# Multi-query attention with exponentials on two engines: the first and the last tiles of VectorE are scheduled otherwise

## The chip, the core and the metric

The kernel runs on one core of a Trainium2 chip. The metric is the device time of one execution in microseconds (us), the median of three runs. A core has TensorE (matrix products), ScalarE (here exponentials), VectorE and GpSimd (elementwise work) and SyncE, which here only starts transfers. The profile calls them PE, ACT, DVE, POOL and SP.

## What is computed

Attention with 16 query heads that share one head of keys and values, for 8 batches of 1024 positions and a head size of 64:

```python
q: (8, 1024, 16, 64)   k, v: (8, 1024, 64)      # float32
scores   = q @ k.T / sqrt(64)
weights  = exp(scores - max(scores))
weights  = weights / sum(weights)
attn_out = weights @ v
```

The kernel leaves out the subtraction of the maximum, which cancels in the division. It gets the sum from two extra columns beside the values, so that one matrix product gives both the weighted values and the sum.

## The kernel before

Heads are taken in 64 pairs. A pair has 8 tiles of 128 keys, so there are 64 x 8 = 512 tiles; a tile has two halves of 512 queries, for both heads: 1024 units of 128 x 1024 scores. TensorE computes a unit with two matmuls into one of three score buffers in PSUM:

```python
sc[t, c] = psp.tile([P, 2, QC], FP32, tag=f"sc{s}", ...)       # s is 0, 1 or 2
for h in range(2):
    nc.tensor.matmul(sc[t, c][:, h, :], <keys>, <queries>, start=True, stop=True, ...)
```

A tile then goes to one of two engines. ScalarE takes one instruction per unit:

```python
ins = nc.scalar.activation(out=w, in_=sc.pop((t, c)), func=EXP, scale=ascale).ins
```

VectorE has no exponential. It writes the scaled score as a 16-bit integer `z` (two instructions per tile, one per unit), whose bits, read as a half-precision number, are a rough power of two. Two corrections are made from it in further steps:

```python
z = scale * score + offset                     # exp_dve: L534, 128 x 1024, reads PSUM
...
steps[t] = (
    e  = z & 0xFC00                            # 0: L551
    m  = z & 1023 | 14 << 10                   # 1: L554
    m  = m * m, the first 1216 columns         # 2: L546; the other 832 by GpSimd in two pieces
    m  = z * m                                 # 3: L558
    m  = m * m, whole                          # 4: L546, in place of 2
    e  = e + m                                 # 5: L560, only for the last tiles
)
```

(The listing is shortened: each line stands for one instruction.) The exponential of such a tile is the sum of three terms, each with a factor. The sum isn't formed; TensorE multiplies each term by values that carry its factor and adds all three up in PSUM:

```python
TERMS = (1.0, 1.017578125, 0.66650390625)
w = (wt[t], zs[t].bitcast(FP16), ms[t])[k] if t in zs else wt[t]
for y in range(x, x + STEP):                   # STEP = 2 matmuls of 128 x 65
    nc.tensor.matmul(acc[p, grp][...], w[...], kst[p // HP]["v"][...][:, j, 0 : D + 1], ...)
```

So a tile on ScalarE costs 16 value matmuls, one on VectorE 48. For each batch the values are scaled for the three terms; in batch 0 VectorE does it, later GpSimd. The products of a pair are collected in three groups (blocks 0 to 6, 6 to 10, 10 to 16), each in one of two accumulators, and VectorE ends a group with a reciprocal (`rec`, L601) and a product (`norm`, L610).

The last 29 tiles (`MERGE`) are treated apart in this version: VectorE squares the whole of `m` itself, adds two of the three terms, and TensorE multiplies only two, one of them by a fourth scaled copy of the last batch's values:

```python
def terms(t):
    return len(TERMS) if t in vtiles and t < NT - MERGE else 1 + (t in vtiles)
```

Which tile goes to which engine, and the order of the instructions on each, comes from `plan`. When the program is built, it goes through the work with estimated durations and always takes next what can start next. Excerpts:

```python
pe = act = dve = 0.0                           # when each engine is free, in the plan
...
if (not vunits and nt < NT - LAST and zfree
        and todo < (BACKLOG if rest > END else BACK_END)):
    vtiles.add(nt)                             # the next tile goes to VectorE
...
n = NT if nt >= NT - SPLIT else nt + 1 if nt > 1 else nt + FIRST
units = [(t, c) for c in range(2) for t in range(nt, n)]      # for ScalarE
...
if free and vunits and gap >= 3 and not zs and dve <= T + PE_L + 0.4 and act > T + ACT_P:
    kind = "z"                                 # the next score is VectorE's
...
lag = min(LAG, END_LAG + (LAG - END_LAG) * rest / END, RAMP * nq / (2 * NKT))
```

At the very start, the first keys and queries are turned on TensorE, and VectorE makes the copies for it (L478 to L500, and L486) ahead of its first step of an exponential.

Of the kernel before, what the change touches and what calls it, by code (L numbers as in the profile page):

```python
# [10 lines left out]
FP16 = mybir.dt.float16  # L11
# [5 lines left out]
P = 128  # L17
ONE = 1024.0
C0 = 0.4578223016
TERMS = (1.0, 1.017578125, 0.66650390625)  # L20
C1, TERMS1 = 0.3051040521, (1.0, 1.52734375)

ACT_P, ACT_L = 0.905, 1.19
QK_P, AV_B, AV_1, SWITCH, PE_L = 0.22, 0.0295, 0.02, 0.10, 0.49
MARGIN, WAIT = 0.318, 0.144
END, END_LAG = 6.0, 0.037
VEC = dict(z=1.13, rec=0.11, val=0.34)
NORM = 0.07, 0.067
STEPS = (0.6, 0.6, 0.7, 1.13)
MERGE, ADD = 29, 1.13  # L30
WHOLE, QUEUE = 1.13, 3
PIECE, PIECE_T, PIECE_AGE = 416, 1.2, 11.627
VEC_L = 0.19
VEC_DEP = 0.12
BACKLOG, BACK_END = 8.353, 2.46
LAST, SPLIT, FIRST = 12, 8, 3
RAMP, VALS, COLD, WARM = 0.584, 3.0, 1, 0.0
BUSY = 20, 3, 5, 0
WBUFS = 23
ZBUFS = 6  # L40
LAG = 2.1
# [4 lines left out]
def follows(x, y):  # L46

    if x is None or y is None:
        return False
    if len(x) == 5:  # L50
        return len(y) == 5 and x[1] == "norm" and y[1] == "rec" and x[2:] == y[2:]
    if len(x) != 2 or len(y) != 2:
        return False
    if y[0] == "z":
        return x in ((y[1], 0), (y[1], 1))
    return x[0] == y[0] and (x[1], y[1]) in ((2, 1), (4, 1), (3, 2), (3, 4), (5, 3))

def plan(NP, NKT, HP=8):

    NT = NP * NKT
    size = [BLOCKS[g + 1] - BLOCKS[g] for g in range(3)]

    def terms(t):
        return len(TERMS) if t in vtiles and t < NT - MERGE else 1 + (t in vtiles)

    def term(t, k):  # L70
        return len(TERMS) if k == 1 and t >= NT - MERGE else k

    def vec(k, g):
        return NORM[0] + NORM[1] * size[g] if k == "norm" else VEC[k]
# [16 lines left out]
            squared.append((t + PIECE_T, x[2]))  # L91

    squared: list = []
    pe = act = dve = 0.0
    mode = ""
    slot = [0.0] * 3
    acc = [0.0] * 2
# [18 lines left out]
    while p < NP or groups:  # L116
        assert min(pe, dve) < 2e3
        if pe <= dve:
            T = pe
            rest = (2 * NT - nq) / (2 * NKT)  # L120
            if not units and nt < NT and (
                len(aring) < WBUFS or used[aring[-WBUFS]] > 2.9
            ):
                todo = (
                    sum(STEPS[n] if n < 4 else ADD for _, n in steps)
                    + sum(vec("norm", x[3]) + vec("rec", x[3]) for x in evs)
                    + VEC["z"] * (len(zs) + len(vunits))
                )
                zfree = len(vring) < ZBUFS or used[vring[-ZBUFS]] > 2.9
                if (  # L130
                    not vunits and nt < NT - LAST and zfree
                    and todo < (BACKLOG if rest > END else BACK_END)
                ):
                    vtiles.add(nt)
                    vring.append(nt)
                    vunits = [(nt, 0), (nt, 1)]
                    ring.append(nt)
                    nt += 1
                n = NT if nt >= NT - SPLIT else nt + 1 if nt > 1 else nt + FIRST
                aring += range(nt, n)  # L140
                ring += range(nt, n)
                units = [(t, c) for c in range(2) for t in range(nt, n)]
                nt = n
            if nt // NKT >= HP * nb - 3 and nb * HP < NP:
                pool += [(T, "val", nb, k) for k in range(len(TERMS) + (HP * (nb + 1) == NP))]
                nb += 1
            cold = COLD if T < WARM else 1
            free = [s for s in range(3) if slot[s] <= T + (SWITCH if mode != "qk" else 0)]
# [11 lines left out]
            for grp in groups:  # L160
                gp, gg, left, a, n, known = grp
                for t in ring[NKT * gp + known : NKT * (gp + 1)]:
                    left += [
                        (t - NKT * gp, k, x) for k in range(terms(t))
                        for x in range(BLOCKS[gg], BLOCKS[gg + 1], STEP)
                    ]
                    grp[5] += 1
                for j, k, x in left:
                    t = NKT * gp + j
                    if t in vtiles:  # L170
                        r = ready.get((t, k, "v"), FAR)
                    else:
                        r = max(ready.get((t, c), FAR) for c in ((0,), (0, 1), (1,))[gg])
                    r = max(r, vdone.get((gp // HP, term(t, k)), FAR))
                    if n == 0:
                        r = max(r, acc[a])
                    if r < tav and (tav > T or grp is groups[0]):
                        tav, pick = r, (grp, (j, k, x))
# [39 lines left out]
            elif do == "av":  # L218
                st = max(T + (SWITCH if mode != "av" else 0), tav)
                pe, mode = st + cost + (AV_1 if mode == "qk" else 0), "av"  # L220
                grp, (j, k, x) = pick
                gp, gg, left, a, n, known = grp
                t = NKT * gp + j
                left.remove((j, k, x))
                end = known == NKT and not left
                emit(st, "av", gp, gg, j, k, x, n, end, a)
                grp[4] += 1
                share = STEP / size[gg] / terms(t)
                nv += share
                used[t] += share  # L230
                if end:
                    acc[a] = FAR
                    evs.append((pe + PE_L, "rec", gp, gg, a))
                    groups.remove(grp)
            else:
                nxt = [x for x in slot + acc + [tav] if T < x < FAR] + [dve] * (dve > T)
                pe = max(min(nxt, default=0.0), T + 1e-3)
        else:
            T = dve
            over = nt >= NT - LAST and not vunits and not zs  # L240
            beside(T, 0.0 if over else PIECE_AGE, ("sq", "val"))
            steps += [(x[1], len(STEPS) - 1) for x in squared if x[0] <= T]
            squared = [x for x in squared if x[0] > T]
            z = [x for x in zs if x[0] <= T + 0.25]
            todo = [("ev", x) for x in evs if x[0] <= T]
            todo += [("val", x) for x in vals if x[0] <= T][:1]
            if nt > NT - MERGE:
                steps.sort()
            todo += [("step", x) for x in steps if x == min(y for y in steps if y[0] == x[0])][:2]
            free = [x for x in todo if not follows(x[1], last)]  # L250
            late = VEC_DEP if not free else 0.0
# [30 lines left out]
                last = None  # L282
            elif what == "step":
                steps.remove(x)
                dve = T + late + (STEPS[x[1]] if x[1] < 4 else ADD)
                if x[1] == len(STEPS) - 2:
                    if x[0] >= NT - MERGE or sum(y[1] == "sq" for y in pool) > QUEUE:
                        x, dve = (x[0], len(STEPS)), T + late + WHOLE
                        steps.append((x[0], len(STEPS) - 1))
                    else:  # L290
                        pool += [(dve, "sq", x[0], n) for n in range(2)]
                emit(T + late, "step", *x)
                if x[0] >= NT - MERGE:
                    if x[1] == 3:
                        steps.append((x[0], 5))
                    elif x[1] == 5:
                        ready[x[0], 0, "v"] = dve + VEC_L
                elif x[1] in (0, len(STEPS) - 1):
                    ready[x[0], x[1] and len(TERMS) - 1, "v"] = dve + VEC_L
                last = x  # L300
            else:
                nxt = [x[0] for x in zs + evs + vals + squared if x[0] > T] + [pe + 1e-6] * (pe > T)
                dve = max(min(nxt, default=0.0), T + 1e-3)
                last = None
# [7 lines left out]
def kernel(  # L312
# [31 lines left out]
        [consts.tile([P, NKT, D + 2], FP16, name=f"vals{i}_{n}") for n in range(len(TERMS))]  # L344
        for i in range(2)
    ]
    NV = NP * NKT - MERGE
    assert NV >= NP * NKT - HP * NKT
    vals[(B - 1) % 2].append(consts.tile([P, NKT, D + 2], FP16, name="vals_last"))
    for x in vals:  # L350
        for y, c in zip(x, TERMS + TERMS1[1:]):
            nc.gpsimd.memset(y[:, :, D : D + 2], c)

    wbuf = [consts.tile([P, 2, S], FP16, name=f"w{i}") for i in range(WBUFS)]
# [41 lines left out]
    def scale_v(b, k, engine):  # L396

        kst[b]["v"] = vals[b % 2]
        return engine.tensor_scalar(
            out=vals[b % 2][k][:, :, 0:D], in0=kst[b]["vn"], scalar1=(TERMS + TERMS1[1:])[k], scalar2=None,  # L400
            op0=ALU.mult)

    def trans_k(b):
# [121 lines left out]
    def exp_dve(t, c):  # L525

        name = f"{t}"  # L530
        if c == 0:
            zs[t] = dvp.tile([P, 2, S], U16, tag="z", bufs=ZBUFS, name=f"z{name}")
        z = zs[t]
        yield nc.vector.tensor_scalar(  # L534
            out=z[:, :, c * QC : (c + 1) * QC], in0=sc.pop((t, c)), scalar1=vscale,
            scalar2=(15 + math.log2(C0 if t < NV else C1)) * ONE, op0=ALU.mult, op1=ALU.add,
        )
        if c == 0:
            return
# [5 lines left out]
        def square(engine, a, b):  # L545
# [3 lines left out]
        squares[t] = square  # L549
        steps[t] = (  # L550
            lambda: V.tensor_scalar(  # L551
                out=wt[t].bitcast(U16), in0=z, scalar1=0xFC00, scalar2=0 if t < NV else 512,
                op0=ALU.bitwise_and, op1=ALU.bitwise_or),
            lambda: V.tensor_scalar(  # L554
                out=m.bitcast(U16), in0=z, scalar1=1023, scalar2=14 << 10,
                op0=ALU.bitwise_and, op1=ALU.bitwise_or),
            lambda: square(V, 0, 2 * S - 2 * PIECE),
            lambda: V.tensor_tensor(out=m, in0=z.bitcast(FP16), in1=m, op=ALU.mult),  # L558
            lambda: square(V, 0, 2 * S),
            lambda: V.tensor_tensor(out=wt[t], in0=wt[t], in1=m, op=ALU.add),  # L560
        )

    def beside(op, t, n):
# [14 lines left out]
    def value(p, grp, j, k, x, n, end, s):  # L578
# [6 lines left out]
        for y in range(x, x + STEP):  # L585
# [1 line left out]
            o = (y - BLOCKS[grp]) * (D + 1)  # L587
            nc.tensor.matmul(  # L588
                acc[p, grp][:, o : o + D + 1], w[:, h, i * P : (i + 1) * P],
                kst[p // HP]["v"][len(TERMS) if k == 1 and t >= NV else k][:, j, 0 : D + 1],  # L590
                start=(n == 0 and y == x), stop=end, skip_group_check=True,
            )

# [123 lines left out]
```

The softmax here doesn't subtract the row's maximum and nothing guards it: scores larger than these inputs give would overflow.

## Time and profile before

| | |
|---|---|
| device time, median of 3 (lowest, highest) | 754.85 us (754.26, 755.1) |
| span of the profiled execution | 753.1 us |
| TensorE matmul / weight load busy | 734.1 us / 490.7 us |
| ScalarE busy | 741.2 us |
| VectorE busy | 708.9 us |
| GpSimd busy | 330.0 us |
| granted TensorE clock | 1.000 |

The span runs from the first to the last instruction of one execution. A line of a timeline gives the start and the duration in us, the engine, the line of the kernel, the operation, what it writes and reads, and in brackets the engine's idle time ahead of it with the instruction that ended the wait. Numbers behind names count the program's buffers: `sc_1_214` is the 214th tile made, a score of the second half (`1`). ScalarE's outputs `w_98` to `w_120` are a ring of 23 buffers.

### The profile page before, as it was taken

The numbers are of one execution on the slowest core, as the hardware profiler recorded it, in microseconds if no ns is written. First come the engines' busy times: TensorE is split into PE (matmuls) and PEld (weight loads), VectorE is DVE, ScalarE is ACT, GpSimd is POOL, SyncE is SP. The second block draws the span as 40 slices with busy tenths as digits, with TensorE's granted clock in tenths as the row PEclk, the third lists the DMA queues.
The fourth block names the chain that finished last, engine by engine and source line by source line (L and its number), as shares of the span: only waits on it lengthen the run. The fifth ranks groups of instructions, "written<-read, shape, count | busy, mean of one in ns | idle before, by whom it ended". The sixth has DMA issues, their size and how long they took to land.

```text
span 753.1 us, 30241 instructions
## 1 busy us (share of the span) xinstructions
PE 734.1 (97%) x13724; PEld 490.7 (65%) x13724; DVE 708.9 (94%) x1054; ACT 741.2 (98%) x808; POOL 330.0 (44%) x392
## 2 busy tenths in 40 slices
PE   7899999999999999999999999999999999999997
PEld 4455666666666666666666666666666666666666
DVE  6999999999999999999999999999999999998973
ACT  7999999999999999999999999999999999999996
POOL 2457434473444643446344563345533457233100
PEclk9999999999999999999999999999999999999999
DMA  7564454646656456674546746458653566643223
GB/s 132 97 108 88 87 105 87 108 95 105 114 108 105 98 83 108 119 122 88 93 77 122 134 86 103 69 108 134 114 92 83 85 128 115 86 93 79 63 71 96
DMA packets 179888, 75.08 MB, mean 100 GB/s; under 512 B 78384, under 2 KB 178736, under 8 KB 179760
## 3 DMA queue, kind: packets, MB, share of 16 engines
q1 hardware_dynamic: 140544, 54.01, 32.4%
q0 software_dynamic: 37744, 18.36, 21.2%
q8 instruction: 107, 1.75, 0.9%
q10 hardware_dynamic: 1472, 0.79, 0.4%
q14 instruction: 21, 0.17, 0.1%
HBM read 39.58 MB, written 33.55 MB: 97 GB/s over the span
## 4 chain that ended last, share of the span: by engine, by line
ACT 94%; PE 3%; DVE 2%; issue 0%; POOL 0%; DVEq 0%; POOLq 0%
ACT w_109 L519 4%; ACT w_110 L519 4%; ACT w_105 L519 4%; ACT w_112 L519 4%; ACT w_115 L519 4%; ACT w_104 L519 4%; ACT w_117 L519 4%; ACT w_116 L519 4%; ACT w_114 L519 4%; ACT w_106 L519 4%; ACT w_118 L519 4%; ACT w_111 L519 4%; ACT w_102 L519 4%; ACT w_113 L519 4%; ACT w_103 L519 4%; ACT w_107 L519 4%
## 5 line engine op out<-in xcount | busy, mean ns | idle before, releaser
L507 PEld LDWEIGHTS <-k2t_137 64*128 64x128 f16 x256 | 13.7, 94 | 19.4 <-issue 11.5
L507 PEld LDWEIGHTS <-k2t_14688 64*128 64x128 f16 x256 | 12.7, 93 | 11.0 <-issue 4.1
L507 PEld LDWEIGHTS <-k2t_1160 64*128 64x128 f16 x256 | 12.3, 93 | 10.7 <-issue 4.3
L507 PEld LDWEIGHTS <-k2t_5644 64*128 64x128 f16 x256 | 12.4, 93 | 8.2 <-issue 1.8
L507 PEld LDWEIGHTS <-k2t_10166 64*128 64x128 f16 x256 | 12.4, 93 | 8.2 <-issue 1.8
L507 PEld LDWEIGHTS <-k2t_7905 64*128 64x128 f16 x256 | 12.4, 93 | 8.2 <-issue 1.8
L507 PEld LDWEIGHTS <-k2t_12427 64*128 64x128 f16 x256 | 12.0, 93 | 8.1 <-issue 1.8
L507 PEld LDWEIGHTS <-k2t_3383 64*128 64x128 f16 x256 | 12.0, 93 | 7.8 <-issue 1.7
L588 PEld LDWEIGHTS <-w_102 128*128 128x128 f16 x288 | 12.9, 97 | 5.4 <-issue 5.4
L588 PEld LDWEIGHTS <-w_106 128*128 128x128 f16 x288 | 13.0, 97 | 4.6 <-issue 4.6
L588 PEld LDWEIGHTS <-w_108 128*128 128x128 f16 x288 | 12.9, 97 | 4.3 <-issue 4.3
L588 PEld LDWEIGHTS <-w_100 128*128 128x128 f16 x288 | 13.0, 97 | 3.9 <-issue 3.9
L588 PEld LDWEIGHTS <-w_104 128*128 128x128 f16 x288 | 12.8, 97 | 4.0 <-issue 4.0
L588 PEld LDWEIGHTS <-w_98 128*128 128x128 f16 x288 | 12.7, 97 | 4.0 <-issue 4.0
L588 PEld LDWEIGHTS <-w_105 128*128 128x128 f16 x288 | 12.8, 97 | 3.4 <-issue 3.4
L588 PEld LDWEIGHTS <-w_119 128*128 128x128 f16 x272 | 12.1, 97 | 4.2 <-issue 4.2
L588 PEld LDWEIGHTS <-w_117 128*128 128x128 f16 x272 | 12.1, 97 | 4.2 <-issue 4.2
L588 PEld LDWEIGHTS <-w_101 128*128 128x128 f16 x288 | 12.7, 97 | 3.1 <-issue 3.1
L588 PEld LDWEIGHTS <-w_99 128*128 128x128 f16 x288 | 12.7, 97 | 3.1 <-issue 2.7
L588 PEld LDWEIGHTS <-w_103 128*128 128x128 f16 x288 | 12.7, 97 | 2.9 <-issue 2.9
L588 PEld LDWEIGHTS <-w_107 128*128 128x128 f16 x288 | 12.6, 97 | 2.9 <-issue 2.9
L588 PEld LDWEIGHTS <-w_110 128*128 128x128 f16 x272 | 12.2, 97 | 3.5 <-issue 3.5
(5591 smaller groups left out, 3706.7 us busy)
## 6 DMA issues: line engine op xcount, KB each, us to landing
qf<-in_q_dram ACTq DMA_DIRECT2D x2, 256.0 KB, 3.7
qn_187<-in_q_dram POOLq DMA_DIRECT2D x1, 512.0 KB, 6.1
qn_328<-in_q_dram POOLq DMA_DIRECT2D x4, 128.0 KB, 3.8
qn_513<-in_q_dram POOLq DMA_DIRECT2D x4, 128.0 KB, 3.0
out_dram<-osb_498 SPq DMA_DIRECT2D x1, 512.0 KB, 3.2
out_dram<-osb_837 SPq DMA_DIRECT2D x1, 512.0 KB, 4.7
qn_1011<-in_q_dram POOLq DMA_DIRECT2D x4, 128.0 KB, 3.1
out_dram<-osb_1151 SPq DMA_DIRECT2D x1, 512.0 KB, 3.2
```

Of the source, the lines that this page charges most:

```text
L507: nc.tensor.matmul(sc[t, c][:, h, :], kst[p // HP]["k2t"][64 * h : 64 * h + 64, key(p // HP, j, h), :], qt[p][64 * h : 64 * h + 64, 4 * c ...
L519: ins = nc.scalar.activation(out=w, in_=sc.pop((t, c)), func=EXP, scale=ascale).ins
L588: nc.tensor.matmul(acc[p, grp][:, o : o + D + 1], w[:, h, i * P : (i + 1) * P], kst[p // HP]["v"][len(TERMS) if k == 1 and t >= NV else k] ...
```

## The change

It undoes the special treatment of the last 29 tiles: no tile of VectorE is merged, all have three terms, the fourth copy of the last batch's values goes, and GpSimd again helps with the squares. This saves VectorE work and lets the plan be simpler. And the plan is told that VectorE is busy with copies until 2.0 in its time, so that ScalarE gets the first three scores and VectorE the fourth; the first scaling of values may be planned from 4.3 on, not from 3.0. The constants that steer the end, the start and the share of VectorE are set anew.

```diff
-C1, TERMS1 = 0.3051040521, (1.0, 1.52734375)
-END, END_LAG = 6.0, 0.037
+END, END_LAG = 5.567, -0.028
-MERGE, ADD = 29, 1.13
-BACKLOG, BACK_END = 8.353, 2.46
-LAST, SPLIT, FIRST = 12, 8, 3
-RAMP, VALS, COLD, WARM = 0.584, 3.0, 1, 0.0
-BUSY = 20, 3, 5, 0
+BACKLOG, BACK_END = 8.576, 2.062
+LAST, SPLIT, FIRST = 13, 7, 3
+RAMP, VALS, COLD, WARM = 0.541, 4.3, 1, 0.0
+BUSY, READY = (20, 3, 5, 0), 2.0
 ...
-    def terms(t):
-        return len(TERMS) if t in vtiles and t < NT - MERGE else 1 + (t in vtiles)
-
-    def term(t, k):
-        return len(TERMS) if k == 1 and t >= NT - MERGE else k
 ...
-    pe = act = dve = 0.0
+    pe, act, dve = 0.0, 0.0, READY
 ...
-                pool += [(T, "val", nb, k) for k in range(len(TERMS) + (HP * (nb + 1) == NP))]
+                pool += [(T, "val", nb, k) for k in range(len(TERMS))]
 ...
-                        (t - NKT * gp, k, x) for k in range(terms(t))
+                        (t - NKT * gp, k, x) for k in range(len(TERMS) if t in vtiles else 1)
 ...
-            over = nt >= NT - LAST and not vunits and not zs
-            beside(T, 0.0 if over else PIECE_AGE, ("sq", "val"))
+            beside(T, PIECE_AGE, ("sq", "val"))
 ...
-            if nt > NT - MERGE:
-                steps.sort()
 ...
-                    if x[0] >= NT - MERGE or sum(y[1] == "sq" for y in pool) > QUEUE:
+                    if sum(y[1] == "sq" for y in pool) > QUEUE:
 ...
-                if x[0] >= NT - MERGE:
-                    if x[1] == 3:
-                        steps.append((x[0], 5))
-                    elif x[1] == 5:
-                        ready[x[0], 0, "v"] = dve + VEC_L
-                elif x[1] in (0, len(STEPS) - 1):
+                if x[1] in (0, len(STEPS) - 1):
                     ready[x[0], x[1] and len(TERMS) - 1, "v"] = dve + VEC_L
 ...
-            lambda: V.tensor_tensor(out=wt[t], in0=wt[t], in1=m, op=ALU.add),
 ...
-                kst[p // HP]["v"][len(TERMS) if k == 1 and t >= NV else k][:, j, 0 : D + 1],
+                kst[p // HP]["v"][k][:, j, 0 : D + 1],
```

More of the change, by code (lines that the diff above doesn't have):

```diff
@@ L55, in follows @@
         return x in ((y[1], 0), (y[1], 1))
-    return x[0] == y[0] and (x[1], y[1]) in ((2, 1), (4, 1), (3, 2), (3, 4), (5, 3))
+    return x[0] == y[0] and (x[1], y[1]) in ((2, 1), (4, 1), (3, 2), (3, 4))
 def plan(NP, NKT, HP=8):
@@ L124, in plan @@
                 todo = (
-                    sum(STEPS[n] if n < 4 else ADD for _, n in steps)
+                    sum(STEPS[n] for _, n in steps)
                     + sum(vec("norm", x[3]) + vec("rec", x[3]) for x in evs)
@@ L173, in plan @@
                         r = max(ready.get((t, c), FAR) for c in ((0,), (0, 1), (1,))[gg])
-                    r = max(r, vdone.get((gp // HP, term(t, k)), FAR))
+                    r = max(r, vdone.get((gp // HP, k), FAR))
                     if n == 0:
@@ L227, in plan @@
                 grp[4] += 1
-                share = STEP / size[gg] / terms(t)
+                share = STEP / size[gg] / (len(TERMS) if t in vtiles else 1)
                 nv += share
@@ L284, in plan @@
                 steps.remove(x)
-                dve = T + late + (STEPS[x[1]] if x[1] < 4 else ADD)
+                dve = T + late + STEPS[x[1]]
                 if x[1] == len(STEPS) - 2:
-                    if x[0] >= NT - MERGE or sum(y[1] == "sq" for y in pool) > QUEUE:
+                    if sum(y[1] == "sq" for y in pool) > QUEUE:
                         x, dve = (x[0], len(STEPS)), T + late + WHOLE
@@ L346 @@
     ]
-    NV = NP * NKT - MERGE
-    assert NV >= NP * NKT - HP * NKT
-    vals[(B - 1) % 2].append(consts.tile([P, NKT, D + 2], FP16, name="vals_last"))
     for x in vals:
-        for y, c in zip(x, TERMS + TERMS1[1:]):
+        for y, c in zip(x, TERMS):
             nc.gpsimd.memset(y[:, :, D : D + 2], c)
@@ L399, in scale_v @@
         return engine.tensor_scalar(
-            out=vals[b % 2][k][:, :, 0:D], in0=kst[b]["vn"], scalar1=(TERMS + TERMS1[1:])[k], scalar2=None,
+            out=vals[b % 2][k][:, :, 0:D], in0=kst[b]["vn"], scalar1=TERMS[k], scalar2=None,
             op0=ALU.mult)
@@ L535, in exp_dve @@
             out=z[:, :, c * QC : (c + 1) * QC], in0=sc.pop((t, c)), scalar1=vscale,
-            scalar2=(15 + math.log2(C0 if t < NV else C1)) * ONE, op0=ALU.mult, op1=ALU.add,
+            scalar2=(15 + math.log2(C0)) * ONE, op0=ALU.mult, op1=ALU.add,
         )
@@ L551, in exp_dve @@
             lambda: V.tensor_scalar(
-                out=wt[t].bitcast(U16), in0=z, scalar1=0xFC00, scalar2=0 if t < NV else 512,
-                op0=ALU.bitwise_and, op1=ALU.bitwise_or),
+                out=wt[t].bitcast(U16), in0=z, scalar1=0xFC00, scalar2=None,
+                op0=ALU.bitwise_and),
             lambda: V.tensor_scalar(
```

## The prediction

> **What bounds the kernel now.** I read the page's busy shares first, then the chain that ended last, then the timelines of ScalarE, TensorE and VectorE at the start, around 70 us and at the end.
>
> ```profile
> PE 734.1 (97%) x13724; PEld 490.7 (65%) x13724; DVE 708.9 (94%) x1054; ACT 741.2 (98%) x808; POOL 330.0 (44%) x392
> ACT 94%; PE 3%; DVE 2%; issue 0%; POOL 0%; DVEq 0%; POOLq 0%
> ```
>
> Three engines look full, so the shares alone don't decide. The chain does: 94% of it is ScalarE, almost all of that exponentials (L519). The ScalarE timeline (start, duration, operation, and in brackets idle time and its releaser) shows how tight that chain is:
>
> ```profile
> 6.48 1.02 ACT L519 ACTIVATE w_98<-sc_0_193 128x1024 f16<-128x1024 f32 x1 [1.29 <-PE sc_0_193 L507]
> ...
> 8.31 1.03 ACT L519 ACTIVATE w_100<-sc_0_211 128x1024 f16<-128x1024 f32 x1
> 9.49 1.02 ACT L519 ACTIVATE w_98<-sc_1_214 128x1024 f16<-128x1024 f32 x1
> ...
> 12.21 1.04 ACT L519 ACTIVATE w_101<-sc_0_239 128x1024 f16<-128x1024 f32 x1
> 13.55 1.02 ACT L519 ACTIVATE w_101<-sc_1_284 128x1024 f16<-128x1024 f32 x1 [0.29 <-PE sc_1_284 L507]
> ...
> 99.72 1.35 ACT L519 ACTIVATE w_102<-sc_0_2049 128x1024 f16<-128x1024 f32 x1
> ...
> 649.86 1.21 ACT L519 ACTIVATE w_103<-sc_0_15591 128x1024 f16<-128x1024 f32 x1
> ...
> 745.74 1.58 ACT L519 ACTIVATE w_109<-sc_1_17958 128x1024 f16<-128x1024 f32 x1
> ```
>
> Durations range from 1.02 to 1.58 us for the same work, so I take the pace from ends. The exponential that ends at 99.72 + 1.35 = 101.07 is number 101, the one that ends at 649.86 + 1.21 = 651.07 is number 701: 550.00 / 600 = 0.9167 us each, with no room between. There are 806; the first ends at 7.50, the last at 747.32. At the pace, 805 steps would take 737.9 us; they took 739.8. So only 1.9 us of the run is ScalarE waiting. Going through all ends, the steps over 0.96 us are four: 1.17 and 1.32 at the start (0.25 + 0.40 lost) and 1.16 and 1.92 near 70 us (0.24 + 1.00 lost). TensorE's timeline says what held them:
>
> ```profile
> 9.06 0.39 PE L507 MATMUL sc_1_214<-qt_134,k2t_137 64*128 64x512 f16 x2 [1.11 <-DVE z_208 L534]
> ...
> 11.50 0.39 PE L507 MATMUL sc_0_239<-qt_134,k2t_137 64*128 64x512 f16 x2 [0.54 <-DVE z_208 L534]
> ...
> 69.28 0.39 PE L507 MATMUL sc_0_1353<-qt_492,k2t_137 64*128 64x512 f16 x2 [0.80 <-DVE z_1319 L534]
> ```
>
> All are scores waiting for VectorE to free a score buffer. At 70 us VectorE was late because two-input operations ran long:
>
> ```profile
> 63.58 1.93 DVE L558 TENSOR_TENSOR m_776<-z_727,m_776 128x2048 f16<-128x2048 f16 x1
> ...
> 69.61 1.76 DVE L558 TENSOR_TENSOR m_870<-z_812,m_870 128x2048 f16<-128x2048 f16 x1
> ```
>
> The end, on TensorE and VectorE:
>
> ```profile
> 744.62 0.39 PE L507 MATMUL sc_1_17958<-qt_16653,k2t_14688 64*128 64x512 f16 x2
> 744.95 0.24 PE L588 MATMUL acc_0_17941<-vals_0_87,w_103 128*128 128x65 f16 x2
> ...
> 747.38 0.24 PE L588 MATMUL acc_1_18002<-vals_0_87,w_109 128*128 128x65 f16 x2 [0.18 <-ACT w_109 L519]
> 747.45 0.34 PE L588 MATMUL acc_2_18041<-vals_0_87,w_102 128*128 128x65 f16 x6
> ...
> 748.73 0.34 PE L588 MATMUL acc_2_18041<-vals_0_87,w_109 128*128 128x65 f16 x6
> ```
>
> After the last score TensorE works off value products until 748.73 + 0.34 = 749.07; then come the last reciprocal and product on VectorE and the output transfer, 4.0 us, to the span's 753.1.
>
> **What the Trainium skill says.** "Perfetto Trace Analysis", Identifying the Most-Contended Engine: the occupancy of ScalarE is a fair measure, matmul busy time isn't. The trace agrees: TensorE's 97% holds waits such as the 1.11 above, ScalarE's 98% doesn't. The same page, Optimizing Scalar/DVE Operations, gives ScalarE about 51 ns of overhead on PSUM; with 1024 elements at the 1.2 GHz of "ScalarE: Activation LUTs" (Specifications) an estimate of 0.904 us. The measured 0.9167 decides. "SBUF — State Buffer", Who interferes with whom: a VectorE operation with two SBUF inputs and a GpSimd operation that reads SBUF exclude each other. The trace fits: the 1.93 us one began 0.06 us after a GpSimd square (63.52, 0.89 us), and alone it takes 1.22 us.
>
> **The change part by part.** It is two things, and the constants of the scheduler are set anew around them.
>
> First, the last 29 key tiles are no longer treated apart. Before, VectorE added two of the three terms there and TensorE multiplied only two by the values. Only 3 of VectorE's tiles (484, 487, 495 of 512) fall there. Removed: three additions of 1.2 us, and three whole squares become partial ones with two GpSimd pieces. Added: 3 x 8 = 24 pairs of value matmuls. VectorE is off the chain at that time (it idles 0.6 to 2.2 us per gap after 731 us), so this removal by itself saves nothing.
>
> Second, the tile split. Laying the instruction orders of the two kernels side by side: VectorE takes 107 tiles, not 109 (214 first steps of 1024-element halves, not 218), so ScalarE has 810 exponentials, not 806. Up to tile 160 both give VectorE 36; it falls behind by one near tile 190 and by another near 340. ScalarE has no slack there: 4 x 0.9167 = **+3.7 us**, wholly on the chain. In return TensorE has 11,616 value matmuls, not 11,632, which is nothing.
>
> Third, the end. After the last score 184 value matmuls stand in the order, not 118, since the third term of tile 496 comes late and the products of its head pair queue behind it. A run of 6 takes 747.45 to 747.63, 0.0304 us each. Before: 118 x 0.0304 = 3.59, of 4.12 us measured from 744.95 to 749.07; the rest is the wait of 0.18, refill and drain. After: 184 x 0.0304 = 5.59, and about 0.25 for drain and changes of group, with no wait for ScalarE, whose last result comes early against this queue: 5.84. Difference **+1.7 us**. The last score is tied to ScalarE by the buffers in both, and what follows the last matmul is the same.
>
> Fourth, the start. The first three scores now all go to ScalarE; VectorE's first comes fourth, when a buffer is freed at about 7.5 us, and VectorE's copy of the queries ends at 7.87 in the profile. Its first step is then done about 9.1, and TensorE isn't kept waiting, as ScalarE has work for three buffers, until about 9.3. Two of the three scalings of values move ahead of its second step, 2 x 0.33 us, which lies before that step's score can arrive (about 10.6). So both waits should go: **-0.65 us**.
>
> Fifth, the wait near 70 us (1.24 us). The order of GpSimd and VectorE work there changes: the first two scalings of the next batch's values follow each other, no longer parted by a query load and squares. Whether two long VectorE operations again meet GpSimd just there is luck; I count half: **-0.6 us**.
>
> Sum: 3.7 + 1.7 - 0.65 - 0.6 = +4.1, so 754.85 + 4.1 = 758.95, say 759.0 us.
>
> **Rivals.** (a) The late VectorE chain at the end costs more than the queue: tile 496's two squares now run on GpSimd (0.87 us each), then VectorE multiplies; if TensorE reaches these products before they are ready, it stands still and keeps ScalarE waiting as well. For it: TensorE takes its orders strictly in turn. Against: ScalarE's real pace is 0.9167 and the scheduler's constant for it is 0.905, so all others have over 1% of slack. It would make some 761. (b) The whole time is bound by TensorE and VectorE as much as by ScalarE, so two tiles fewer on VectorE relieve them and the four exponentials come for nothing. TensorE at 97% speaks for it, the steady pace without waits against it. It would make some 755. (c) The new order brings other collisions of VectorE with GpSimd; each that stops a score costs up to 1 us, as at 70 us: 760 to 762. (d) The start gains and the collisions vanish fully, and the end costs only half: some 757.5.
>
> **Range and chances.** The 3.7 us is the surest term, as it is a count times a measured pace. Start and end have errors of some 0.5 us each, the collisions of about 1 us on either side with more room above. That gives 757.0 to 761.5. Both limits lie within 1% of 754.85, and 2% would be 15 us, which nothing here can bring: faster 0.01, within 2% 0.97, slower 0.02.
>
> **What would show it.** Right: the page has ACT x812 in place of x808, ends of exponentials still 0.9167 us apart in the middle, the chain still over 90% ScalarE, no step above 0.96 us before 14 us, and some 5.8 us from the first value product after the last score to the last one. Wrong: steps over 0.96 us in new places with VectorE as releaser (c), TensorE waiting after 720 us for the product of the last VectorE tile (a), or a pace other than 0.9167 (b). If ScalarE's last exponential ends before 747.3, the count of exponentials wasn't what mattered, and the prediction is wrong at its root.

## The result, and the profile after

The changed kernel takes 761.7 us (four runs, 760.83 to 762.38) where the kernel before takes 754.56: a ratio of 1.0093, 95% interval 1.0076 to 1.0111. It is slower by 7.1 us. I had predicted 4.1 more and a range up to 761.5, so the time lies just above the range and the cost is well above what I gave.

First the lines of the page that answer to those of before: busy shares, and the chain that ended last.

```profile
PE 731.3 (96%) x13708; PEld 490.4 (65%) x13708; DVE 700.5 (92%) x1039; ACT 745.3 (98%) x812; POOL 340.3 (45%) x392
...
ACT 72%; PE 18%; DVE 9%; issue 0%; POOL 0%; POOLq 0%
```

ScalarE has the four exponentials more that were counted (812 in place of 808 instructions), and VectorE and TensorE have less to do. Yet the chain now runs through TensorE and VectorE for 27% of the span. That is the sign that something besides ScalarE's count took part. ScalarE's timeline shows where:

```profile
6.33 1.02 ACT L498 ACTIVATE w_96<-sc_0_191 128x1024 f16<-128x1024 f32 x1 [1.28 <-PE sc_0_191 L486]
...
31.55 1.02 ACT L498 ACTIVATE w_109<-sc_1_534 128x1024 f16<-128x1024 f32 x1 [0.38 <-PE sc_1_534 L486]
...
98.96 1.27 ACT L498 ACTIVATE w_100<-sc_0_2024 128x1024 f16<-128x1024 f32 x1
...
190.55 1.35 ACT L498 ACTIVATE w_104<-sc_0_4222 128x1024 f16<-128x1024 f32 x1
...
444.63 1.35 ACT L498 ACTIVATE w_104<-sc_1_10414 128x1024 f16<-128x1024 f32 x1
446.41 1.02 ACT L498 ACTIVATE w_105<-sc_0_10440 128x1024 f16<-128x1024 f32 x1 [0.42 <-PE sc_0_10440 L486]
...
533.15 1.02 ACT L498 ACTIVATE w_106<-sc_0_12506 128x1024 f16<-128x1024 f32 x1 [0.47 <-PE sc_0_12506 L486]
...
537.12 1.02 ACT L498 ACTIVATE w_108<-sc_0_12592 128x1024 f16<-128x1024 f32 x1 [0.20 <-PE sc_0_12592 L486]
...
750.38 1.56 ACT L498 ACTIVATE w_109<-sc_1_17852 128x1024 f16<-128x1024 f32 x1
```

Ends, as before: exponential 101 ends at 100.23, number 201 at 191.90, so 0.9167 us each, the same pace. Before 31 us no step is long: the waits of the old start are gone. But there are new ones: 0.47 us over the pace at 31 us, 0.15 at 261, 0.53 at 446, and 0.57, 0.30 and 0.21 between 533 and 538. An end is compared with the end before it, so 446.41 + 1.02 - (444.63 + 1.35) - 0.92 = 0.53.

The end on TensorE:

```profile
749.25 0.39 PE L486 MATMUL sc_1_17852<-qt_16577,k2t_14576 64*128 64x512 f16 x2
749.57 0.30 PE L565 MATMUL acc_2_17843<-vals_0_87,w_118 128*128 128x65 f16 x4
...
755.07 0.34 PE L565 MATMUL acc_2_18007<-vals_0_87,w_109 128*128 128x65 f16 x6
```

From the first value product after the last score to the last one: 755.07 + 0.34 - 749.57 = 5.84 us, what the prediction had from 184 matmuls. That it agrees to the hundredth is luck, as 0.25 us of the 5.84 was a rough allowance.

The two profiled executions, which took 754.85 and 761.9 us, differ by 7.05 us. The parts, rounded:

| part | predicted | measured in the profiles |
|---|---|---|
| four exponentials more | +3.7 | +3.67 |
| value products after the last exponential | +1.7 | +1.72 |
| ScalarE waits at the start | -0.65 | -0.65 |
| ScalarE waits near 70 us | -0.6 | -0.5 (1.24 before, 0.73 after) |
| ScalarE waits at 261, 446, 533 to 538 us | none | +1.8 |
| ScalarE wait at 31 us | none | +0.5 |
| first exponential ends earlier | none | -0.15 |
| from the last matmul to the end of the span | 0 | +0.4 |
| outside the span | 0 | +0.3 |

The four predicted rows hold. The two rows of waits that I had not put in make 2.3 us, and the experiments are about them. The row of 0.4 us, output transfers, need not be of the change: three later kernels with just the same end have 3.97 to 4.3 us there, the profile after 4.4 and the one before 4.0. The last row is steady, 2.1 us outside the span in each of the four runs and 1.7 to 2.0 in the runs of the kernel before, but no view explains it.

### The profile page after: what moved, and what is told of

Its sections match the earlier page's. It is cut to its first block, busy times and chain, and to the rows that moved or that the text cites. A ratio compares the mean times of both kernels' runs of the same rounds, so it can differ in the third digit from the quotient of the medians.

```text
span 759.8 us, 30200 instructions
## 1 busy us (share of the span) xinstructions
PE 731.3 (96%) x13708; PEld 490.4 (65%) x13708; DVE 700.5 (92%) x1039; ACT 745.3 (98%) x812; POOL 340.3 (45%) x392
## 4 chain that ended last, share of the span: by engine, by line
ACT 72%; PE 18%; DVE 9%; issue 0%; POOL 0%; POOLq 0%
ACT w_99 L498 3%; ACT w_98 L498 3%; ACT w_112 L498 3%; ACT w_97 L498 3%; ACT w_100 L498 3%; ACT w_96 L498 3%; ACT w_111 L498 3%; ACT w_113 L498 3%; ACT w_101 L498 3%; ACT w_105 L498 3%; ACT w_106 L498 3%; ACT w_115 L498 3%; ACT w_110 L498 3%; ACT w_114 L498 3%; ACT w_109 L498 3%; ACT w_116 L498 3%
## 5 line engine op out<-in xcount | busy, mean ns | idle before, releaser
L486 PEld LDWEIGHTS <-k2t_12326 64*128 64x128 f16 x256 | 12.6, 93 | 10.7 <-issue 4.1
```

Of the source, the lines that this page charges most:

```text
L486: nc.tensor.matmul(sc[t, c][:, h, :], kst[p // HP]["k2t"][64 * h : 64 * h + 64, key(p // HP, j, h), :], qt[p][64 * h : 64 * h + 64, 4 * c ...
```

## The experiments

All times are compared with runs of the kernel before in the same session, which varied between 754.0 and 757.8 us; why is told under the hardware. "Waits" are ScalarE's steps above the pace of 0.9167 us, added up.

**1. Merging alone taken out.** The first part of the change on the kernel before; the fourth copy of the last batch's values is still made.

```diff
-MERGE, ADD = 29, 1.13
+MERGE, ADD = 0, 1.13
```

> The kernel before with the merging of the last 29 tiles taken out and nothing else changed. Its order of instructions has 804 exponentials on ScalarE (806 before) and 248 value matmuls after the last score (118 before). Theory of counts: 2 x 0.9167 = 1.8 us less on ScalarE, and an end of 248 x 0.0304 + 0.25 = 7.8 us in place of 4.1, so 3.7 more: 754.6 + 1.9 = 756.4 us. Theory that most of the loss comes from VectorE and GpSimd meeting at other places: the count of exponentials and the end explain less than half of the difference, and the time is over 758 us. If merging made no difference, 754.6.

Measured 759.17 us, ratio 1.0043 (1.0031 to 1.0055). 804 exponentials and 248 matmuls in 7.79 us are as counted, but one new wait of 1.46 us stands at 732 us. TensorE, then VectorE, of this run:

```profile
732.13 1.08 PE L588 MATMUL acc<-vals,w 128*128 128x65 f16 x30 [1.55 <-DVE osb L610]
```

```profile
727.87 1.74 DVE L558 TENSOR_TENSOR m<-z,m 128x2048 f16<-128x2048 f16 x1
729.53 0.18 DVE L601 RECIPROCAL rec<-acc 128x6 f32<-128x6 f32 x1
730.38 1.23 DVE L558 TENSOR_TENSOR m<-z,m 128x2048 f16<-128x2048 f16 x1 [0.67 <-POOL m L546]
731.52 0.55 DVE L610 TENSOR_TENSOR osb<-acc,rec 128x384 f32<-128x384 f32 x1
```

TensorE waits for an accumulator, as the product that ends a group (731.52) stands behind a step of the last tile, which waits for GpSimd's square. This is my rival (a), in this kernel. The changed kernel doesn't have it: no step more than 0.05 us over the pace after 540 us. The wait is real, then, but other constants of the end keep clear of it. And merging alone is worth more than its 24 pairs of matmuls: without it the queue at the end is twice as long. That this is because the third term comes late is read from the order, and not tested.

**2. The new start alone.**

```diff
-RAMP, VALS, COLD, WARM = 0.584, 3.0, 1, 0.0
-BUSY = 20, 3, 5, 0
+RAMP, VALS, COLD, WARM = 0.541, 4.3, 1, 0.0
+BUSY, READY = (20, 3, 5, 0), 2.0
 ...
-    pe = act = dve = 0.0
+    pe, act, dve = 0.0, 0.0, READY
```

> The kernel before with the new start alone (VectorE planned as busy until 2.0, scaling of values from 4.3, the ramp constant of the changed kernel); merging stays. Its order has 810 exponentials (806) and 136 value matmuls after the last score (118). Theory of counts: +3.7 us for the exponentials, +0.3 us for the end, -0.65 us for the waits at the start: 754.6 + 3.3 = 757.9 us. Theory of collisions: on top of that 1 to 2.5 us of ScalarE waiting at new places, 759 to 760.5. A start that only gains would give 753.9.

Measured 761.43 us, ratio 1.0070 (1.0056 to 1.0083), near the changed kernel and above both theories. The waits are 0.16 us at 261, 0.53 at 446, 0.58, 0.31 and 0.22 at 533 to 538 us: the same as in the changed kernel, to 0.01 us. So the two tiles fewer and the waits in the middle of the run both come from the start, up to half a millisecond earlier; the end of the kernel has no part in them. Counts and new waits add, but they are not the whole 7.0 us of the profiled execution (761.87 against 754.85 us): 3.7 us are exponentials, 0.8 more waits in all, 1.0 more after the last exponential, and 1.6 more outside the span. There the six runs have 2.1 to 3.4 us, so that the time comes so near the changed kernel's is in part chance.

**3. The scaling of values left out, changed kernel.** Values of batches 2 to 7 are not scaled, their products use those of batch 0 or 1.

```diff
-            ins = scale_v(t, n, nc.gpsimd)
 ...
+            kst[t]["v"] = vals[t % 2]
+            ins = scale_v(t, n, nc.gpsimd) if t < 2 or n == 3 else None
```

> The changed kernel without the scaling of the values of batches 2 to 7 on GpSimd; their products take the scaled values of batch 0 or 1. The profile of the changed kernel has ScalarE waits near 261, 446 and 533 to 538 us, 0.15 + 0.53 + 1.08 = 1.8 us in all, each beside such a scaling. Theory of collisions: they vanish, 761.7 - 1.8 = 759.9 us, and the one near 31 us stays. If VectorE is late there for another cause (its own order), they stay: 761.7.

(There is no copy with `n == 3` in the changed kernel.) Measured 759.94 us. All waits from 100 us on are gone; those at 29 to 31 (0.35 us) and near 73 us (0.74) stay. The chain of this run is ScalarE's again:

```profile
ACT 91%; PE 6%; DVE 2%; POOL 0%; issue 0%; POOLq 0%
```

One of the places, VectorE, GpSimd and TensorE in the changed kernel, then VectorE with the scaling left out:

```profile
441.33 1.18 DVE L512 TENSOR_SCALAR z_10331<-sc_0_10318 128x1024 uint16<-128x1024 f32 x1
442.43 0.54 DVE L587 TENSOR_TENSOR osb_10177<-acc_2_10191,rec_2_10322 128x384 f32<-128x384 f32 x1
442.89 1.48 DVE L524 TENSOR_TENSOR m_10230<-m_10230 128x1216 f16<-128x1216 f16 x1
444.30 1.21 DVE L536 TENSOR_TENSOR m_9910<-z_9799,m_9910 128x2048 f16<-128x2048 f16 x1
```

```profile
441.39 1.49 POOL L378 TENSOR_SCALAR vals_2_89<-vn_9782 128x512 f16<-128x512 f32 x1 [0.63 <-DVE m_10230 L532]
442.85 0.88 POOL L524 TENSOR_TENSOR m_10093<-m_10093 128x416 f16<-128x416 f16 x1
```

```profile
445.57 0.36 PE L565 MATMUL acc_0_10294<-vals_2_86,m_9910 128*128 128x65 f16 x6 [0.68 <-DVE m_9910 L536]
...
445.98 0.39 PE L486 MATMUL sc_0_10440<-qt_9780,k2t_7841 64*128 64x512 f16 x2
```

```profile
442.33 0.78 DVE L524 TENSOR_TENSOR m<-m 128x1216 f16<-128x1216 f16 x1
443.03 1.22 DVE L536 TENSOR_TENSOR m<-z,m 128x2048 f16<-128x2048 f16 x1
```

The square takes 1.48 us where a GpSimd square begins 0.04 us ahead of it, and 0.78 us alone: 0.70 us lost. It is the exclusion that the Trainium skill's "SBUF — State Buffer", Who interferes with whom, describes for a VectorE operation with two SBUF inputs and a GpSimd operation that reads SBUF, and the traces agree with it: 1.48 us against 0.78. The GpSimd square begins just there as it follows the scaling, which ends at 442.88, without a gap. The multiplication behind VectorE's square is late, and so is the value product that takes it, for which TensorE waits 0.68 us; the next score, and the exponential at 446.41, are late with it.

**4. Early scores twice, changed kernel.** This is about the wait at 31 us. The 20th to 35th score are computed twice into the same buffer.

```diff
-        for h in range(2):
+        for h in (0, 1) * (2 if 20 <= scores[0] < 36 else 1):
```

> The changed kernel in which the 20th to 35th score are computed twice into the same buffer, so that TensorE has more to do between 20 and 29 us. In the changed kernel TensorE's granted clock is half from about 28 to 31 us and ScalarE waits 0.47 us at 31 us; its runs with a mean clock of 1.000 and of 0.995 were 1.5 us apart. Theory that the thin work there brings the clock down: the clock stays 1.000, the wait at 31 us goes, the time is 761.7 - 0.7 = 761.0 us and the spread between its runs gets smaller. If the clock has another cause, it drops as before and the time is 761.7 or a little more.

Measured 761.12 us (760.92 to 761.33), clock 0.999 or 1.000 in all five runs, no wait at 31 us. Busy time by stretch, first the changed kernel, then this one (TensorE, its weight loads, VectorE, ScalarE, GpSimd, then granted clock, share of the transfer engines, GB/s):

```profile
24.50:28.00 3.50, 1.83 (x13) 0.60 (x13) 3.50 (x4) 3.50 (x5) 1.93 (x3) 0.99 0.65 80
28.00:31.50 3.50, 3.50 (x36) 1.90 (x36) 3.04 (x7) 3.18 (x4) 1.93 (x3) 0.52 0.26 48
```

```profile
24.50:28.00 3.50, 2.61 (x20) 0.94 (x19) 3.50 (x4) 3.50 (x5) 1.94 (x3) 1.00 0.56 70
28.00:31.50 3.50, 3.50 (x60) 2.19 (x58) 3.43 (x7) 3.50 (x5) 2.10 (x3) 1.00 0.54 104
```

With 1.83 us of TensorE work between 24.5 and 28 us, the next 3.4 us run at half clock, and ScalarE is short of 0.32 us there; with 2.61 us they don't. The kernel before had 2.31 us between 24.5 and 28 us and kept its clock. The spread of the runs fell from 1.55 to 0.41 us. The median is 0.6 us lower, which the intervals (1.0058 to 1.0082 here) don't separate from the changed kernel.

**5. Control: scaling left out of the kernel before** (the edit of 3; the fourth copy for the last batch is still made).

> The kernel before without the scaling of the values of batches 2 to 7 on GpSimd (only the fourth copy for the last batch is still made); products take the scaled values of batch 0 or 1. Control for the same step in the changed kernel. The kernel before has no ScalarE wait over 0.1 us beside those scalings, so the time should stay: 754.9, within 0.3 us. If leaving the scaling out relieved VectorE in general, it would gain 1.9 us as the changed kernel did.

Measured 754.72 us, ratio 0.9994 (0.9986 to 1.0003). Nothing to gain there: the scaling costs the kernel before nothing, and the changed one 1.8 us. That is not because VectorE and GpSimd never meet in the kernel before. VectorE, then GpSimd, of its profile, where ScalarE has no wait:

```profile
441.82 1.23 DVE L554 TENSOR_SCALAR m_10387<-z_10281 128x2048 uint16<-128x2048 uint16 x1
```

```profile
441.62 0.87 POOL L546 TENSOR_TENSOR m_10235<-m_10235 128x416 f16<-128x416 f16 x1
```

This step takes 0.68 us alone. Taking all steps of VectorE between 100 and 700 us that ran more than 0.1 us over the usual time of their kind, I estimate that VectorE lost some 7 us in the kernel before, 9.5 in the changed one, 6 with the scaling left out there, and 1 in this run. Only the changed kernel, of these four, turned any of it into waits of ScalarE in that stretch. So what the changed kernel lacked was not freedom from collisions, but room for them.

**6. Both edits on the changed kernel** (3 and 4 together).

> The changed kernel with both edits: scaling of batches 2 to 7 left out, and the 20th to 35th score computed twice. Both waits that I did not foresee should be gone and only the counts left: against the kernel before +3.7 us for four exponentials, +1.7 us for the end, -0.65 us for the start, -0.5 us near 70 us: 754.9 + 4.2 = 759.1 us. If the four exponentials cost nothing by themselves, it would be 755.4.

Measured 759.35 us (759.06 to 759.46), ratio 1.0052 (1.0037 to 1.0067). Only the waits near 73 us are left (0.74 us). This is the prediction's kernel, as it were: with the two unforeseen causes taken out, the sum expected here holds to 0.25 us. The comparison is kind to it, as all six runs had a clock of 1.000: against those runs of the kernel before that had it too (median 754.44), the difference is 4.9 us in place of 4.2, and 0.3 of that lies outside the span. That four exponentials come for nothing, rival (b), is out.

**7. One constant of the changed kernel.**

```diff
-RAMP, VALS, COLD, WARM = 0.541, 4.3, 1, 0.0
+RAMP, VALS, COLD, WARM = 0.49, 4.3, 1, 0.0
```

> The changed kernel with one constant of the plan otherwise: RAMP, which says how fast value products may be planned at the start, 0.49 in place of 0.541. With it the tiles of VectorE fall at the same places in each batch 2 to 6 (in the changed kernel no two of these batches are alike), there are 804 exponentials in place of 810 and 224 value matmuls after the last score in place of 184. Theory that the lost tiles and the collisions come from the order that does not repeat: -5.5 us for 6 exponentials, +1.2 us for 40 matmuls, -1.8 us as the waits at 261, 446 and 533 to 538 us don't come: 761.7 - 6.1 = 755.6 us, up to 757 if a wait for the last VectorE tile comes as it did at 732 us where merging alone was taken out. If the waits come from the scaling itself, wherever it lies, they are there again: 757.4 or more.

Measured 756.01 us, ratio 1.0011 (1.0001 to 1.0020). 5.7 us come back from a constant that acts in the first pairs. In the kernel before, the tiles of VectorE in each of the batches 2 to 6 are 1, 7, 10, 15, 18, 23, 30, 33, 39, 42, 47, 50, 55, 62 of 64. In the changed kernel they are 5, 8, 14, 17, ... in batch 2 and 0, 7, 10, 15, 21, ... in batch 3; no two batches agree, and two of the five have 13 tiles, not 14. With 0.49 they are the list of the kernel before again. All three scalings per batch are made, and no wait over 0.1 us comes after 75 us. So neither the scaling nor the later first step of VectorE costs the time by itself, but the order that the start sets off. VectorE still loses some 7 us to collisions between 100 and 700 us, as in the kernel before; why that order has room for them and the other has not, no run shows.

**8. A version meant to beat both.** Merging, the new start, and constants with few exponentials and a short queue.

```diff
-RAMP, VALS, COLD, WARM = 0.584, 3.0, 1, 0.0
+RAMP, VALS, COLD, WARM = 0.49, 4.3, 1, 0.0
-END, END_LAG = 6.0, 0.037
+END, END_LAG = 7.622, 0.138
-MERGE, ADD = 29, 1.13
+MERGE, ADD = 39, 1.13
-BACKLOG, BACK_END = 8.353, 2.46
+BACKLOG, BACK_END = 9.329, 4.453
```

(and READY as in 2)

> A version meant to beat both: the kernel before with merging (last 39 tiles), the new start, RAMP 0.49 and other constants for the end. 804 exponentials and 172 value matmuls after the last score, tiles at the same places in each batch 2 to 6. Theory of counts: against the kernel before -1.8 us for two exponentials, +1.4 us for the end (172 x 0.0304 + 0.25 = 5.5 in place of 4.1), -0.65 us for the start, 0 to -1.2 us for the waits near 70 us: 752.7 to 753.9 where the kernel before takes 754.9. Theory of collisions: new ones at places that cannot be told, 754 to 757.

Measured 755.25 us, ratio 1.0000 (0.9991 to 1.0009). Exponentials, queue (5.48 us) and first waits are as counted. The gain went into 0.6 us of waits up to 32 us, at half clock for 10 us, 1.9 us at 69 to 72 us, and 0.36 at 476 us.

**9 and 10. Against these waits:** early scores twice (16th to 39th) and the three scalings of batch 1 planned 8 us apart, on version 8 and on the kernel before.

```diff
-                pool += [(T, "val", nb, k) for k in ...]
+                pool += [(T + (8.0 * k if nb == 1 else 0.0), "val", nb, k) for k in ...]
```

> The version f2 (merging, new start, RAMP 0.49) with two more edits: the 16th to 39th score computed twice, to keep TensorE's clock up, and the three scalings of the values of batch 1 planned 8 us apart on GpSimd in place of two at once. In f2 the half clock lasts 10 us, with 0.6 us of ScalarE waits by 32 us, and 1.9 us of waits lie at 69 to 72 us beside two scalings in a row (3.46 us of GpSimd). If both causes are right, the waits go: 755.2 - 0.6 - 1.9 = 752.8 us, clock 1.000. If the spaced scalings only meet other VectorE steps, half comes back: 753.7. If the waits have another cause, 755.2.

> The kernel before with the same two edits (16th to 39th score twice, scalings of batch 1 planned 8 us apart), nothing else. The waits of 1.25 us at 69 to 72 us should go or shrink to half, and with the clock held, its runs should all be as the quick ones (754.3) less that: 753.1 us, up to 753.7. If the waits have another cause, 754.3.

Measured 754.92 us, ratio 0.9997 (0.9990 to 1.0005), and 756.37 us, ratio 1.0024 (1.0016 to 1.0032). Both missed. In the first the clock held and the waits at 69 to 72 us are gone, but one of 1.16 us is now at 84 us, where TensorE, then VectorE, show:

```profile
84.26 0.36 PE L588 MATMUL acc<-vals,m 128*128 128x65 f16 x6 [1.07 <-DVE m L558]
```

```profile
81.03 2.04 DVE L554 TENSOR_SCALAR m<-z 128x2048 uint16<-128x2048 uint16 x1
82.99 1.21 DVE L558 TENSOR_TENSOR m<-z,m 128x2048 f16<-128x2048 f16 x1
```

A step of 0.68 us takes 2.04 beside GpSimd work there. Moving the scalings moved the collision. In the second, small waits (1.5 us) came between 20 and 35 us, where scores are doubled; in the profiled run the clock fell already at 10.7 us, and the waits before 16 us are 1.9 us in place of 0.6. Of those near 70 us, 0.7 us stay at 72 to 75 us and 0.5 us come at 90 us. No version here beats the kernel before.

## Why the prediction was wrong, by its own steps

*What bounds the kernel:* right. One reading on the way was not: the 1.11 us that TensorE waits are idle time, and no part of its 97%. ScalarE's pace is 0.9167 us before and after, and in experiments 3 and 6 it accounts for over 90% of the chain. The check "chain still over 90% ScalarE" failed for the changed kernel itself, and this pointed to the cause.

*First, the merging:* that its removal "by itself saves nothing" is right, but it isn't a small thing: experiment 1 costs 3.5 us, though it has two exponentials fewer. I read the part from the order of the whole change, where other constants had already repaired it.

*Second, the split:* right. Four exponentials, 3.67 us; six fewer and the order back in step bring 5.7 us back in experiment 7, after 40 more matmuls at the end are paid for. That VectorE "falls behind by one near tile 190 and by another near 340" was seen, and not asked about; it was the trace of an order out of step.

*Third, the end, and fourth, the start:* right in size, 1.72 and -0.65 us.

*Fifth, the collisions:* this step failed. It looked only where the kernel before had a wait, near 70 us, and counted half of that as a gain, which came out nearly so (-0.5). For all the rest of the run it took the kernel before's freedom from waits over to a kernel with another order. I had it as rival (c), "each that stops a score costs up to 1 us", and gave it no term in the sum. Measured: 1.8 us of waits at three places beside GpSimd's scalings, shown by experiments 3, 5 and 7. The argument used against rival (a), that ScalarE's real pace gives the others over 1% of slack, holds on average and says nothing of a single step of VectorE that takes twice its time.

*Not foreseen at all:* the half clock at 28 us, 0.5 us in the profiled execution. The changed kernel's one run with a clock of 1.000 took 760.83 us, inside the range. The cause is shown by experiment 4, its size in the median is not resolved.

Of rival (a), the 1.5 us wait exists in experiment 1 and not in the changed kernel. The 0.3 us outside the span stay open.

## What to carry to other kernels

Where a schedule is planned ahead and one engine is full, count its instructions and the queue that is left behind its last one: both terms came out to 0.1 us. Then ask whether the new order still repeats from batch to batch as the tuned one did; an order in which collisions cost nothing is not inherited when a constant of the first microseconds shifts all that follows. Give the waits a term in the sum, and more room above than below.

## What the runs showed of the hardware

TensorE's clock fell to half in the middle of a busy kernel, without a long idle time: between 24.5 and 28 us in the changed kernel the longest idle time of TensorE is 0.53 us. The stretches at half clock last 3.4, 6.8 or 10.2 us, and whether they come differs from run to run, as the mean clocks of one kernel, 0.995 to 1.000, tell. In each of the seven profiles with such a fall, the 3.4 us just ahead of it hold 1.76 to 2.16 us of TensorE work, less than any other such stretch since the clock last rose. No sharp limit comes out: experiment 1 kept its clock with 2.01 us. The Trainium skill's "TensorE: Matmul & The Clock Gate", What's actually happening, tells of a free-running window of about 3.4 us, which fits, and of a clock set by how busy TensorE has been, which fits too; the idle window that its table gives as the cause isn't what the trace has.

The clock goes with the spread of the kernel before: of its 35 runs beside experiment 7, those with a mean clock of 1.000 took 754.1 to 755.0 us, those with 0.998 took 754.8 to 755.8, those with 0.995 took 756.6 to 757.8. In the kernel of experiment 7 it hardly matters: seven of eight runs with 0.995 took 755.8 to 756.3 us, those with 0.998 took 755.8 to 756.1.

VectorE's steps with a single input (128 x 2048) ran long beside GpSimd as well: 2.04 us for one of 0.68 in experiment 9, more than the loss of the two-input square (1.48 for 0.78).
